# Output projection's first tiles inside the end of attention, and the embeddings' second operands in tiles of their own

## The chip, the cores and the metric

The kernel runs on one core of one Trainium2 chip. The metric is the time of one execution on the device in microseconds: 3075.62 us, the median of three runs (3073.82 to 3077.36). Lower is better.

## The reference

Two layers of an encoder over 1024 tokens of width 1024, all in fp32. Layer 0 mixes tokens by two groups of heads side by side (dilated windows, and attention with latent keys and values), layer 1 by differential attention. With `mix(x)` the heads' outputs side by side, a layer is

```
x <- LN(alpha*x + mix(x) @ W_o)          # output projection, then layer norm
x <- LN(alpha*x + convGLU(x))
x <- x + sigmoid(x @ W_g) * (p[i] @ W_p) # per-layer embeddings, p[i] is 1024 x 256
```

The change touches the last attention items of both layers, the output projection behind them, and `p[i] @ W_p`, which is worked out ahead of time among the last attention items.

## The kernel before, in words

**Operands.** For a product in fp32, each operand is split into a rounded high part (`...h`) and a low remainder (`...l`), and each block is three matmuls: high by high, high by low, low by high (`mm3`, L159 to L161). `split` (L146, or L139 by `pool_copy`) makes the high part on GpSimd (POOL) or, where the call says so, on ScalarE (ACT); the low part is a subtraction on VectorE (DVE, L149). `load_split` (L153) loads a matrix into a raw tile and splits it. Raw tiles of a region come in two rotating buffers. At the end of attention they serve, in turn, the embeddings' operands `wpr` and `ppr`, the eight weights of the output projection `wor` (tiles `woh`, `wol` after the split), and the mix rows `mr` (`mhl` after the split). A load waits on SP, the queue that issues transfers, until the low part of the buffer's last user is made.

**Attention.** A layer's attention is a row of items, 128 in layer 0 and 64 in layer 1; one is a head and a tile of 128 query rows. `a()` makes scores `s`, the row maximum `nmx` on DVE, and the exponential `e` on ACT (L440) with its sum. In layer 0, `r` (a reciprocal on DVE) and a multiplication on POOL (L740) norm `e`; in layer 1, two exponentials are combined with POOL (L845) and DVE (L846). `b()` transposes `e` on TensorE into `xt` (L164) and splits that to `pth`, `ptl`. `c()`, once for two items, multiplies by the values into `av` (L447, L448), and `d()` writes the outputs `oT`. `pipeline` calls these in an order one item apart, and runs at each item's slot what a plan has put there. `last_plan` fills that plan for the last head: the load of the embeddings' operands, 16 products `pe` of 128 x 512, the eight weights, and, at the last slot (`end - MT_SLOT[i]`, with zero for both layers), the load and split of the mix rows of tile 0 (`MixTiles.seven`, seven of eight heads; the last head comes from `oT`).

**Output projection.** `out_proj` goes over eight tiles of 128 tokens. A tile is 48 matmuls (8 heads, 2 halves of 512, 3 products) into one of the two PSUM buffers of two banks, which it shares with the attention scores (`banks2`). Behind it come the residual (DVE, L1078), the sums of the layer norm (DVE, L892; their sum L895; POOL L896 and L897 for the root), two passes on DVE (L902, L903) and one on POOL (L904), a store `xmid`, and in `xt.put` eight transposes of `xn` (L164) with their splits `xb` on ACT and DVE, which feed the next stage. The transposes of tile t - 1 are written behind the matmuls of tile t.

**Order.** Each engine runs its own list in a fixed order. A scheduler of the framework sets these lists from the order of the code and its own estimates. The two rotating raw buffers, and the pools' buffers in general, decide which instruction waits for which.

Of the kernel before, what the change touches and what calls it, by code (L numbers as in the profile page):

```python
# [15 lines left out]
P = 128  # L16
NT = 8
NK = 8
# [5 lines left out]
LAM_INIT = 0.8 - 0.6 * math.exp(-0.3)  # L24
N_UNITS = 36
PE_SLOTS = ((15, 5, 0), (6, 1, 0))
MT_SLOT = (0, 0)
DOWN = ("a00", "s4", "a01", "s2", "s3", "s1", "a11")
AHEAD = 3

# [2 lines left out]
def tile_hybrid_encoder(  # L33
# [32 lines left out]
    nc = tc.nc  # L66
# [33 lines left out]
    region = [None]  # L100
# [24 lines left out]
    def banks2(s):  # L125
        return ps.tile([P, 1024], F32, tag="s", name=nm(s), bufs=2)
# [21 lines left out]
            pool_copy(h, raw)  # L148
        (lo or nc.vector).tensor_tensor(l, raw, f32(h), op=ALU.subtract)  # L149

    def load_split(dram, shape, s, make=runit, hi=None, lo=None):
        r = region[0].raw(s + "r", shape)
        nc.sync.dma_start(out=r, in_=dram)  # L153
        h, l = make(s + "h", shape), make(s + "l", shape)
        split(r, h, l, hi, lo)
        return h, l
# [311 lines left out]
            for step in self.at.get((slot, place), ()):  # L468
                step()

    def pipeline(items, plan):


        n = len(items)
        items[0].prep()
        items[1].prep()
        items[2].prep()
        plan.run(-1, "first")
        items[0].a()
        plan.run(-1, "last")  # L480
        pending = ended = None
        for i in range(n):
            plan.run(i, "first")
            if i + 1 < n:
                items[i + 1].a()
            if i + 3 < n:
                items[i + 3].prep()
            plan.run(i, "mid")
            if ended is not None:
                ended.d()  # L490
                ended = None
            if pending is not None:
                pending.c()
                pending, ended = None, pending
            items[i].b()
            if items[i].t % 2 == 1:
                pending = items[i]
            plan.run(i, "last")
        pending.c()
        pending.d()  # L500

# [405 lines left out]
    class MixTiles:  # L907

        def __init__(self, i):
            self.i, self.m = i, {}  # L910

        def seven(self, t):

            mr = region[0].raw("mr", [P, NK, P])
            nc.sync.dma_start(out=mr[:, 0:7, :], in_=mix[self.i].rearrange("k p q -> p k q")[:, 0:7, t * P:(t + 1) * P])
            two = [runit("mhl", [P, 2, 4, P]) for _ in range(2)]
            for j, m in enumerate(two):
                n = 4 - j
                split(mr[:, 4 * j:4 * j + n], m[:, 0, 0:n], m[:, 1, 0:n])
            self.m[t] = mr, two  # L920

        def last(self, t, oT):
            mr, two = self.m[t]
            x = oT[:, t * P:(t + 1) * P]
            split(x, two[1][:, 0, 3], two[1][:, 1, 3], nc.scalar)
            self.m[t] = [(two[k // 4][:, 0, k % 4], two[k // 4][:, 1, k % 4]) for k in range(NK)]

    def last_plan(plan, i, first, end):


        w, wp, pp = [], [], []

        def load():
            new_region(4)
            for k in range(2):
                wp.append(load_split(w_pp[i, k], [P, 1024], "wp", rtile))
                pp.append(load_split(pT_in[i, :, k, :], [P, 1024], "pp", rtile if k == 0 else runit))

        def project(t, n):
            ts, sl = slice(t * P, t * P + P), slice(512 * n, 512 * n + 512)  # L940
            pe = bank("pe")
            for k in range(2):
                mm3(pe, pp[k][0][:, ts], pp[k][1][:, ts], wp[k][0][:, sl], wp[k][1][:, sl], k == 0, k == 1)
            for h in range(2):
                o = mid1("peo", [P, 256])
                nc.scalar.copy(o, pe[:, 256 * h:256 * h + 256])
                nc.sync.dma_start(out=pes[i][t, :, 512 * n + 256 * h:512 * n + 256 * h + 256], in_=o)

        def weight(k):
            w.append(load_split((w_abo, w_co)[i][k], [P, 1024], "wo", rtile if k > 4 else runit))  # L950

        mid, late, hold = PE_SLOTS[i]
        plan.add(first - 1, "mid", load)
        for t in range(NT):
            for n in range(2):
                j = 2 * t + n
                slot = end if j >= 16 - hold else first + j * mid // (16 - hold)
                plan.add(slot, "mid", lambda t=t, n=n: project(t, n))
        for k in range(NK):
            plan.add(first + late + k * (end - first - late) // NK, "mid", lambda k=k: weight(k))  # L960
        mt = MixTiles(i)
        plan.add(end - MT_SLOT[i], "mid", lambda: mt.seven(0))
        return w, mt

    def mixer_ab(xt):
        mask = big("mask", [P, 1664])
        st = {}
        last = {}

        def sink(i):  # L970
            def f(oT):
                if i < 7:
                    nc.sync.dma_start(out=mix[0][i], in_=oT)
                last["oT"] = oT
            return f

        ablk = [Block64(xt, w_a[i], True) for i in range(4)]
        new_region(3)
        xt.begin(0, ablk[0])
        for t in range(1, 4):  # L980
            xt.load(t)
        xt.split(1)
        rope_tables()
        for t in range(NT):
            if t + 4 < NT:
                xt.load(t + 4)
            if t == 2:
                constants()
            if t == 4:
                nc.sync.dma_start(out=mask, in_=mask_in)  # L990
            if t + 2 < NT:
                xt.split(t + 2)
            ablk[0].project(t, 2)
        ablk[0].keys(NT - 2)
        cT = Latent(xt)
        grp = [GroupB(cT, g) for g in range(2)]
        bblk = [BlockB(cT, grp[i // 2], i) for i in range(4)]
        items, plan = [], Plan()
        for i in range(4):
            sti = {"sink": sink(i)}  # L1000
            items += [ItemA(ablk[i], j, t, mask, sti) for j in range(2) for t in range(NT)]
            if i < 3:
                ablk[i + 1].plan(plan, 16 * i - 1, 2)
            else:
                plan.add(16 * i - 1, "mid", lambda: cT.load(384, w_cq))
                plan.spread(cT.steps() + bblk[0].steps(), 16 * i, 16 * i + 13)
                plan.add(16 * i + 14, "mid", lambda: bblk[0].keys(NT - 1))
        for i in range(4):
            sti = {"sink": sink(4 + i)}
            items += [ItemB(bblk[i], j, t, sti) for j in range(2) for t in range(NT)]  # L1010
            if i < 3:
                plan.spread(bblk[i + 1].steps(), 64 + 16 * i, 64 + 16 * i + 13)
                plan.add(64 + 16 * i + 14, "mid", lambda i=i: bblk[i + 1].keys(NT - 1))
            else:
                w, mt = last_plan(plan, 0, 112, 127)
        plan.add(-1, "first", lambda: ablk[0].keys(NT - 1))
        plan.add(-1, "last", lambda: ablk[1].load(True), lambda: ablk[1].project(0))
        pipeline(items, plan)
        return w, mt, last["oT"]

    def mixer_c(xt, late):
# [24 lines left out]
                w, mt = last_plan(plan, 1, 56, 63)  # L1046
        plan.add(-1, "first", lambda: blk[0].keys(NT - 1))
        plan.add(-1, "last", lambda: blk[1].load(True), lambda: blk[1].project(0))
        pipeline(items, plan)
        return w, mt, last["oT"]  # L1050


    def out_proj(i, w, mt, oT, xsrc, xt, early):

        ln = LN(ln_mg[i], ln_mb[i])
        xns, m = [], mt.m

        def load(t):
            if t < NT:
                if t not in m:  # L1060
                    mt.seven(t)
                mt.last(t, oT)
# [3 lines left out]
            nc.sync.dma_start(out=xns[t], in_=xsrc[t])  # L1066

        def linear(t, beside=None):

            xr, mt_ = xns[t], m.pop(t)  # L1070
            po = banks2("po")
            for k in range(NK):
                if k == NK // 2 and beside:
                    beside()
                for n in range(2):
                    sl = slice(512 * n, 512 * n + 512)
                    mm3(po[:, sl], *mt_[k], w[k][0][:, sl], w[k][1][:, sl], k == 0, k == NK - 1)
            nc.vector.scalar_tensor_tensor(xr, xr, ALPHA, po, op0=ALU.mult, op1=ALU.add)  # L1078

        load(0)  # L1080
        for t in range(NT):
            residual(t)
            load(t + 1)
            if t < NT - 1:
                linear(t)
            else:
                early(0)
                linear(t, lambda: early(1))
                ln(xns[t], True)
                nc.sync.dma_start(out=xmid[i][t], in_=xns[t])  # L1090
            if t:
                xt.put(t - 1, xns[t - 1])
            if t < NT - 1:
                ln(xns[t], t == NT - 2)
                nc.sync.dma_start(out=xmid[i][t], in_=xns[t])
# [624 lines left out]
```

## Time and profile before

| | us |
|---|---|
| median of three runs | 3075.62 (3073.82 to 3077.36) |
| profiled execution | 3070.2, of it the span 3068.4 |
| TensorE busy | 2956.1 (96% of the span) |
| VectorE busy | 2339.5 (76%) |
| ScalarE, GpSimd busy | 1239.0, 1110.6 |
| mean granted TensorE clock | 0.99 of full speed |
| end of layer 0's attention, its output projection | about 690 to 704, 703 to 812 |
| layer 1's embeddings | about 2116 to 2180 |
| end of layer 1's attention, its output projection | about 2180 to 2200, 2195 to 2307 |

A row of the timeline has the start, the duration, the engine, the line, the operation with its tiles by the program's names, the shapes, and the count where equal instructions follow each other. In brackets stands the time for which the engine had been idle before it and what ended that. PE is TensorE, SPq the queue of transfers. Matmuls overlap, so the time from one start to the next is shorter than the duration shown. A row of windows has the length, the busy time of PE, its weight loads, DVE, ACT and POOL with counts, the granted clock, and the share and rate of transfers.

### The profile page before, as it was taken

The page shows a single profiled execution, that of the slowest core. Times are in us where ns is not written, and L with a number is a line of the kernel's source. Part 1 is how long each engine was busy: PE and PEld are TensorE (multiplying, and loading weights), DVE is VectorE, ACT ScalarE, POOL GpSimd, SP SyncE. Part 2 cuts the span into 40 slices and gives each one's busy share as a digit, 9 for nine tenths or more (in the row PEclk, how much of TensorE's full clock was granted, in tenths as well). Part 3 has the DMA queues.
Part 4 walks back from the last instruction along what each step waited for, and adds up shares of the span by engine and source line. Part 5 has one row for each costly group of instructions (what it writes and reads, how often), then busy time and mean ns, then how long its engine had stood idle before and what let it go on. Part 6 is the DMA issues. An engine that isn't in the chain of part 4 may idle for free.

```text
span 3068.4 us, 43192 instructions
## 1 busy us (share of the span) xinstructions
PE 2956.1 (96%) x15456; PEld 2535.4 (83%) x15456; DVE 2339.5 (76%) x4014; ACT 1239.0 (40%) x2652; POOL 1110.6 (36%) x1646
## 2 busy tenths in 40 slices
PE   8999999999889999999999999999998999999989
PEld 8888989887778888877788999998776888887877
DVE  6676477876898888788638777777779988879674
ACT  5555477761232222223226555555413322222221
POOL 4444544333232222234225555554333222213232
PEclk9999999999999999999999999999998999999999
DMA  3000100033223232734111100001532232255331
GB/s 122 29 28 19 38 29 8 22 118 130 96 103 103 99 106 106 283 112 168 56 59 36 35 28 29 28 18 62 174 108 86 103 103 103 103 201 198 97 137 65
DMA packets 119718, 272.14 MB, mean 89 GB/s; under 512 B 11344, under 2 KB 35024, under 8 KB 119504
## 3 DMA queue, kind: packets, MB, share of 16 engines
q1 hardware_dynamic: 119504, 269.37, 25.6%
q8 instruction: 123, 2.02, 0.3%
q14 instruction: 91, 0.75, 0.1%
HBM read 196.46 MB, written 72.88 MB: 88 GB/s over the span
## 4 chain that ended last, share of the span: by engine, by line
PE 70%; DVE 16%; issue 6%; POOL 3%; ACT 3%; DMA 2%; SPq 0%; POOLq 0%; DVEq 0%; ACTq 0%
PE xt L164 5%; PE pb L159 5%; PE pb L160 5%; PE pb L161 5%; PE pp L159 4%; PE s L588 4%; PE pp L161 4%; PE pp L160 4%; PE pd L160 2%; PE pd L161 2%; PE pd L159 2%; PE pa L159 2%; PE pg L159 2%; PE pa L161 2%; PE pa L160 2%
## 5 line engine op out<-in xcount | busy, mean ns | idle before, releaser
L142 DVE TENSOR_TENSOR ptl<-xt,pth 128x512 fp32r<-128x512 f32 (+2 forms) x384 | 239.7, 652 | 59.2 <-ACT pth L399 42.6
L159 PE MATMUL pp<-wh,xth 128*128 128x384 f32 x768 | 266.3, 347 | 7.9 <-ACT wh L146 7.4
L160 PE MATMUL pp<-wl,xth 128*128 128x384 f32 x768 | 258.8, 337 | 1.9 <-DVE wl L149 1.9
L161 PE MATMUL pp<-wh,xtl 128*128 128x384 f32 x768 | 257.9, 336 | 0.0
L440 ACT ACTIVATE e<-s,nmx 128x1024 f32<-128x1024 f32 x192 | 214.7, 1120 | 81.4 <-DVE nmx L838 58.7
L160 PE MATMUL pd<-wd,gd 128*128 128x512 f32 x616 | 242.4, 393 | 4.2 <-DVE wd L142 4.2
L159 PE MATMUL pd<-wd,gd 128*128 128x512 f32 x616 | 241.0, 391 | 0.0
L161 PE MATMUL pd<-wd,gd 128*128 128x512 f32 x616 | 240.5, 390 | 0.0
L139 POOL TENSOR_SCALAR wd<-wd 128x512 fp32r<-128x512 f32 x154 | 129.9, 848 | 290.8 <-PE pd L161 215.6
L1149 ACT CAST gd<-gr 128x512 fp32r<-128x512 f32 x154 | 94.8, 622 | 312.2 <-PE pd L161 222.0
L325 ACT CAST w<-ws 128x512 fp32r<-128x512 f32 x132 | 81.2, 621 | 336.8 <-PE pb L161 281.2
L164 PE MATMUL xt<-ident,e 128*128 128x128 f32 x1440 | 198.0, 274 | 10.0 <-POOL e L740 3.0
L159 PE MATMUL pb<-xt,w 128*128 128x512 f32 x528 | 207.0, 392 | 0.0
L160 PE MATMUL pb<-xt,w 128*128 128x512 f32 x528 | 206.5, 391 | 0.0
L161 PE MATMUL pb<-xt,w 128*128 128x512 f32 x528 | 206.3, 391 | 0.0
L139 POOL TENSOR_SCALAR w<-ws 128x512 fp32r<-128x512 f32 x44 | 33.4, 761 | 467.1 <-PE pa L161 416.9
L164 PEld LDWEIGHTS xt<-ident,e 128*128 128x128 f32 x1440 | 163.4, 141 | 30.7 <-ACT sq L870 5.9
L142 DVE TENSOR_TENSOR wd<-wd,wd 128x512 fp32r<-128x512 f32 x154 | 112.3, 731 | 68.8 <-POOL wd L139 68.8
L142 DVE TENSOR_TENSOR w<-ws,w 128x512 fp32r<-128x512 f32 x176 | 152.4, 869 | 5.2 <-ACT w L325 3.2
L159 PEld LDWEIGHTS pp<-wh,xth 128*128 128x128 f32 x768 | 144.6, 188 | 13.4 <-ACT wh L146 8.0
L838 DVE TENSOR_REDUCE nmx<-s 128x1 f32<-128x1024 f32 x128 | 150.4, 1213 | 1.7 <-PE s L588 1.6
L159 PE MATMUL pb<-xb,w 128*128 128x512 f32 x352 | 140.2, 398 | 9.8 <-DVE u L1330 5.7
(293 smaller groups left out, 8864.5 us busy)
## 6 DMA issues: line engine op xcount, KB each, us to landing
gr<-gated SPq DMA_DIRECT2D x76, 512.0 KB, 3.7
gated<-c SPq DMA_DIRECT2D x90, 256.0 KB, 3.7
wf<-in_w_gate_dram SPq DMA_DIRECT2D x44, 512.0 KB, 4.0
wf<-in_w_up_dram SPq DMA_DIRECT2D x44, 512.0 KB, 4.1
wd<-in_w_down_dram SPq DMA_DIRECT2D x44, 512.0 KB, 6.0
wr<-in_w_c_dram SPq DMA_DIRECT2D x32, 384.0 KB, 3.2
gated<-u SPq DMA_DIRECT2D x44, 256.0 KB, 2.2
pes<-peo SPq DMA_DIRECT2D x64, 128.0 KB, 1.9
```

The source lines that it names most:

```text
L139: nc.gpsimd.tensor_scalar(o, i, 1.0, 1.0, op0=ALU.mult, op1=ALU.mult)
L142: nc.vector.tensor_tensor(lo, src, f32(hi), op=ALU.subtract)
L159: nc.tensor.matmul(o, lhsT=lh, rhs=rh, start=start, stop=False)
L160: nc.tensor.matmul(o, lhsT=lh, rhs=rl, start=False, stop=False)
L161: nc.tensor.matmul(o, lhsT=ll, rhs=rh, start=False, stop=stop)
L164: nc.tensor.transpose(o, in_=i, identity=ident)
L325: nc.scalar.copy(h, v)
L440: nc.scalar.activation(dst, s, AF.Exp, bias=negmax, scale=1.0, accum_out=l)
L588: nc.tensor.matmul(s[:, kh * 512:kh * 512 + 512], lhsT=qt[:, hl, i, :], rhs=self.ks[kh][:, j, :], start=hl == 0, stop=hl == 1)
L838: nc.vector.tensor_reduce(out=nmx, in_=s, axis=AX.X, op=ALU.max, negate=True)
L1149: nc.scalar.copy(g[:, 0], rg)
```

## The change

Two things change. First, the output projection's work starts inside the attention. The mix rows of tile 0 are loaded two slots earlier and those of tile 1 at the last slot. `pipeline` takes a function `tail`: heads 0 to 3 of tile 0 (24 matmuls) are written ahead of the last item's transposes, heads 4 to 6 (18) ahead of the last pair's values. Behind the attention, heads 0 to 6 of tile 1 (42) come first, then head 7 of tile 0, then head 7 of tile 1; later tiles are as before. Second, the embeddings' second operands are loaded into tiles of the unit pool and no longer into the rotating raw buffers; the high part of the second weight moves from POOL to ACT, and the tile pools of the second `pp` stay as they were.

```diff
-MT_SLOT = (0, 0)
...
-    def load_split(dram, shape, s, make=runit, hi=None, lo=None):
-        r = region[0].raw(s + "r", shape)
+    def load_split(dram, shape, s, make=runit, hi=None, lo=None, raw=None):
+        r = (raw or region[0].raw)(s + "r", shape)
...
-    def pipeline(items, plan):
+    def pipeline(items, plan, tail):
...
+            if i == n - 1:
+                tail(0)
             items[i].b()
             if items[i].t % 2 == 1:
                 pending = items[i]
             plan.run(i, "last")
+        tail(1)
         pending.c()
         pending.d()
...
+        def part(self, t, ks):
+
+            if t not in self.po:
+                self.po[t] = banks2("po")
+            for k in ks:
+                h, l = (self.two[t][k // 4][:, a, k % 4] for a in range(2))
+                for n in range(2):
+                    sl = slice(512 * n, 512 * n + 512)
+                    mm3(self.po[t][:, sl], h, l, self.w[k][0][:, sl], self.w[k][1][:, sl], k == 0, k == NK - 1)
+
+        def tail(self, n):
+
+            self.part(0, range(4) if n == 0 else range(4, 7))
...
             for k in range(2):
-                wp.append(load_split(w_pp[i, k], [P, 1024], "wp", rtile))
-                pp.append(load_split(pT_in[i, :, k, :], [P, 1024], "pp", rtile if k == 0 else runit))
+                raw = unit if k else None
+                wp.append(load_split(w_pp[i, k], [P, 1024], "wp", rtile, nc.scalar if k else None, raw=raw))
+                pp.append(load_split(pT_in[i, :, k, :], [P, 1024], "pp", runit if k else rtile, raw=raw))
...
-        plan.add(end - MT_SLOT[i], "mid", lambda: mt.seven(0))
+        plan.add(end - 2, "mid", lambda: mt.seven(0))
+        plan.add(end, "mid", lambda: mt.seven(1))
+        mt.w = w
...
         def linear(t, beside=None):
-
-            xr, mt_ = xns[t], m.pop(t)
-            po = banks2("po")
-            for k in range(NK):
-                if k == NK // 2 and beside:
+            xr = xns[t]
+            if t > 1:
+                mt.part(t, range(4))
+                if beside:
                     beside()
-                for n in range(2):
-                    sl = slice(512 * n, 512 * n + 512)
-                    mm3(po[:, sl], *mt_[k], w[k][0][:, sl], w[k][1][:, sl], k == 0, k == NK - 1)
+                mt.part(t, range(4, 7))
+            mt.part(t, (7,))
+            m.pop(t)
+            po = mt.po.pop(t)
             nc.vector.scalar_tensor_tensor(xr, xr, ALPHA, po, op0=ALU.mult, op1=ALU.add)
...
             load(t + 1)
+            if t == 0:
+                mt.part(1, range(7))
```

The line numbers of the profile are those of the kernel before; in the changed kernel the splits and matmuls stand one line higher, the layer norm two lower, and the residual at L1096. Three places of the instruction order show what moves.

GpSimd at the end of layer 0's attention, before (the last three weights, `e` of the last two items, the mix rows of tile 0 and tile 1):

```order
L740 TENSOR_SCALAR e_9440<-e_9440,r_9438 128x1024
L139 TENSOR_SCALAR woh_9334<-wor_9332 128x1024
L139 TENSOR_SCALAR woh_9387<-wor_9385 128x1024
L740 TENSOR_SCALAR e_9488<-e_9488,r_9486 128x1024
L139 TENSOR_SCALAR woh_9459<-wor_9457 128x1024
L139 TENSOR_SCALAR mhl_9545<-mr_9543 128x512
L139 TENSOR_SCALAR mhl_9546<-mr_9543 128x384
```

and now:

```order
L742 TENSOR_SCALAR e_9440<-e_9440,r_9438 128x1024
L138 TENSOR_SCALAR woh_9334<-wor_9332 128x1024
L138 TENSOR_SCALAR woh_9387<-wor_9385 128x1024
L138 TENSOR_SCALAR woh_9459<-wor_9457 128x1024
L138 TENSOR_SCALAR mhl_9465<-mr_9463 128x512
L138 TENSOR_SCALAR mhl_9466<-mr_9463 128x384
L742 TENSOR_SCALAR e_9496<-e_9496,r_9494 128x1024
```

The last item's `e` has moved behind the last weight and the mix rows of tile 0. On TensorE its transposes have 24 matmuls of tile 0 ahead of them.

TensorE in layer 0's output projection, around the transposes of tile 0's `xn`, before (`po_9676` is tile 1, `po_9776` tile 2):

```order
L159 MATMUL po_9676<-woh_9459,mhl_9595 128x512
L160 MATMUL po_9676<-wol_9460,mhl_9595 128x512
L161 MATMUL po_9676<-woh_9459,mhl_9595 128x512
L164 MATMUL xt_9734<-ident,xn_9590 128x128 x4
L164 MATMUL xt_9743<-ident,xn_9590 128x128 x4
L159 MATMUL po_9776<-woh_8950,mhl_9668 128x512
```

and now:

```order
L160 MATMUL po_9776<-woh_9133,mhl_9711 128x512
L158 MATMUL po_9776<-woh_9257,mhl_9712 128x512
L159 MATMUL po_9776<-wol_9258,mhl_9712 128x512
L163 MATMUL xt_9734<-ident,xn_9641 128x128 x4
L163 MATMUL xt_9743<-ident,xn_9641 128x128 x4
L160 MATMUL po_9776<-woh_9257,mhl_9712 128x512
```

The transposes stand 26 matmuls into tile 2; tile 0 itself now ends six matmuls before tile 1 does. Those of tile 1's `xn` stand 14 matmuls into tile 3, those of tile 2's 4 into tile 4, and from tile 3 on the order is as before. Layer 1 has the same.

VectorE there, before (`xn_9590` is tile 0, `xn_9664` tile 1):

```order
L1078 SCALAR_TENSOR_TENSOR xn_9590<-xn_9590,po_9602 128x1024
L892 BN_STATS st_9652<-xn_9590 128x6 x2
L895 BN_AGGR mv_9653<-st_9652 128x2
L902 TENSOR_SCALAR xn_9590<-xn_9590,mv_9653,rs_9654 128x1024
L903 TENSOR_TENSOR xn_9590<-xn_9590,lngb_9585 128x1024
L1078 SCALAR_TENSOR_TENSOR xn_9664<-xn_9664,po_9676 128x1024
L142 TENSOR_TENSOR xb_2369_9728<-xt_9734,xb_2367_9726 128x2x128
```

and now (tile 0 is `xn_9641`, tile 1 `xn_9707`):

```order
L1096 SCALAR_TENSOR_TENSOR xn_9641<-xn_9641,po_9559 128x1024
L894 BN_STATS st_9695<-xn_9641 128x6 x2
L1096 SCALAR_TENSOR_TENSOR xn_9707<-xn_9707,po_9645 128x1024
L897 BN_AGGR mv_9696<-st_9695 128x2
L904 TENSOR_SCALAR xn_9641<-xn_9641,mv_9696,rs_9697 128x1024
L905 TENSOR_TENSOR xn_9641<-xn_9641,lngb_9636 128x1024
L141 TENSOR_TENSOR xb_2369_9728<-xt_9734,xb_2367_9726 128x2x128
```

The residual of tile 1 stands inside the layer norm of tile 0, between its sums and their sum; the sums of tile 1 follow the splits of tile 0's transposes in both.

More of the change, by code (lines that the diff above doesn't have):

```diff
@@ L909, in __init__ @@
         def __init__(self, i):
-            self.i, self.m = i, {}
+            self.i, self.m, self.two, self.po = i, {}, {}, {}
+        def part(self, t, ks):
[8 more added lines that the diff above has]
+            self.part(0, range(4) if n == 0 else range(4, 7))
         def seven(self, t):
@@ L919, in seven @@
                 split(mr[:, 4 * j:4 * j + n], m[:, 0, 0:n], m[:, 1, 0:n])
-            self.m[t] = mr, two
+            self.m[t] = self.two[t] = two
         def last(self, t, oT):
-            mr, two = self.m[t]
+            two = self.two[t]
             x = oT[:, t * P:(t + 1) * P]
             split(x, two[1][:, 0, 3], two[1][:, 1, 3], nc.scalar)
-            self.m[t] = [(two[k // 4][:, 0, k % 4], two[k // 4][:, 1, k % 4]) for k in range(NK)]
     def last_plan(plan, i, first, end):
@@ L1017, in mixer_ab @@
         plan.add(-1, "last", lambda: ablk[1].load(True), lambda: ablk[1].project(0))
-        pipeline(items, plan)
+        pipeline(items, plan, mt.tail)
         return w, mt, last["oT"]
@@ L1048, in mixer_c @@
         plan.add(-1, "last", lambda: blk[1].load(True), lambda: blk[1].project(0))
-        pipeline(items, plan)
+        pipeline(items, plan, mt.tail)
         return w, mt, last["oT"]
```

## The prediction

> **What bounds the kernel now.** I read the page's first two parts, then TensorE's timeline around the three places that the change touches, then those of the engines that release it there.
>
> ```profile
> span 3068.4 us, 43192 instructions
> PE 2956.1 (96%) x15456; PEld 2535.4 (83%) x15456; DVE 2339.5 (76%) x4014; ACT 1239.0 (40%) x2652; POOL 1110.6 (36%) x1646
> 694.24 1.04 PE L164 MATMUL xt<-ident,e 128*128 128x128 f32 x8
> 697.57 1.10 PE L164 MATMUL xt<-ident,e 128*128 128x128 f32 x8 [2.29 <-POOL e L740]
> 698.90 0.39 PE L447 MATMUL av<-pth,v 128*128 128x256 f32 x1 [0.24 <-ACT pth L399]
> 699.63 0.38 PE L448 MATMUL av<-ptl,v 128*128 128x256 f32 x1 [0.34 <-DVE ptl L142]
> 702.60 0.63 PE L159 MATMUL po<-woh,mhl 128*128 128x512 f32 x1
> 2185.86 0.63 PE L164 MATMUL xt<-ident,e 128*128 128x128 f32 x4 [2.75 <-ACT e L440]
> 2193.28 1.09 PE L164 MATMUL xt<-ident,e 128*128 128x128 f32 x8 [2.06 <-DVE e L846]
> 2133.39 1.38 PE L159 MATMUL pe<-wph,pph 128*128 128x512 f32 x3 [1.03 <-POOL pph L139]
> ```
>
> TensorE is busy 96% of the span, so only what fills or opens its gaps counts. The gaps meant here are short: 2.87 us at layer 0's last item (2.29 + 0.24 + 0.34), 4.81 in the two rows of layer 1's, 1.03 for the second operand of the embeddings. One more resource shows in the granted clock, by windows of 3.41 us:
>
> ```profile
> 696.73:700.14 3.41, 1.99 (x13) 1.56 (x14) 2.53 (x5) 1.27 (x3) 1.83 (x2) 1.00 0.90 287
> 700.14:703.56 3.42, 3.42 (x16) 3.23 (x16) 2.88 (x5) 0.70 (x3) 1.31 (x2) 0.50 0.58 180
> 2130.33:2133.74 3.41, 1.31 (x5) 0.79 (x6) 3.41 (x4) 1.21 (x2) 2.37 (x2) 1.00 0.31 119
> 2133.74:2137.15 3.41, 3.41 (x9) 2.46 (x8) 3.27 (x4) 0.10 (x1) 0.00 (x0) 0.50 0.48 155
> 2181.53:2184.94 3.41, 1.58 (x9) 1.07 (x7) 3.41 (x6) 1.86 (x5) 2.01 (x1) 1.00 0.54 127
> 2184.94:2188.35 3.41, 2.22 (x17) 2.01 (x18) 3.41 (x5) 0.82 (x2) 1.04 (x1) 1.00 0.88 284
> ```
>
> (After the colon pair: length, busy PE, PEld, DVE, ACT, POOL, then the clock.) After windows with gaps the clock is 0.50 for one window, which costs 1.7 us; 1.31 us of work brought it on, 1.58 us in layer 1 did not.
>
> **Layer 0's end of attention.** New there: 24 matmuls of tile 0 ahead of the last item's transposes. They need the mix rows.
>
> ```profile
> 696.18 0.38 SPq L915 DMA_DIRECT2D mr<-mix  x1
> 693.52 2.63 DVE L149 TENSOR_TENSOR wol<-wor,woh 128x1024 fp32r<-128x1024 f32 x2
> 701.33 2.33 SPq L915 DMA_DIRECT2D mr<-mix  x2
> 700.95 1.31 POOL L139 TENSOR_SCALAR mhl<-mr 128x512 fp32r<-128x512 f32 x2 [1.32 <-DMA mr<-mix]
> 705.08 1.10 POOL L139 TENSOR_SCALAR mhl<-mr 128x512 fp32r<-128x512 f32 x2 [2.82 <-DMA mr<-mix]
> ```
>
> The load of the mix rows waits for a raw slot, which weight 6's low part frees at 696.15. Two planner slots earlier do not move that: the issue stays at 696.18, the rows are there 4.77 us later. Their first hi half is split by 700.95 + 0.65 = 701.6. So TensorE, free of transposes at 695.03 (694.24 and eight steps of 0.1, as from 724.87 to 725.66 below), stands 6.6 us; the third matmul waits another 0.45 for DVE's low half; and the window to 703.56 runs at half clock, 0.75 more: 7.8 lost. Before, 702.60 - 695.03 = 7.57 held eight transposes (0.8) and 16 av matmuls of half the width of po's (0.12 each), 2.7 us at full clock, so 4.9 were lost, and 0.4 to 703.56: 5.3. **+2.5 us**. The last e, now behind both mix splits on POOL, comes at about 704.3 (702.3, the two low parts and r on DVE, 1.1 for e). The 24 matmuls last 5.5 us, to 707 and more (48 from 725.66 to 736.79 give 0.23 a step), so it is late for nobody. Bounds: +2.0 if the rows land in 3.75 us, as the next tile's do, from the issue at 701.33 to the split at 705.08; +4.2 with a second half-clock window.
>
> By the Trainium skill (TensorE: Matmul & The Clock Gate, Part 1: The HAM clock gate) the clock halves after an idle window of about 3.4 us; a standstill of 6.6 contains one, so rule and row make the same half-clock window, and it cannot be saved here.
>
> **Layer 1's end.**
>
> ```profile
> 2182.15 0.33 SPq L153 DMA_DIRECT2D wor<-in_w_co_dram  x1
> 2183.31 1.21 DVE L838 TENSOR_REDUCE nmx<-s 128x1 f32<-128x1024 f32 x1
> 2184.55 1.11 ACT L440 ACTIVATE e<-s,nmx 128x1024 f32<-128x1024 f32 x1 [1.54 <-DVE nmx L838]
> 2193.74 1.48 DVE L149 TENSOR_TENSOR mhl<-mr,mhl 128x512 fp32r<-128x512 f32 x2
> ```
>
> Here the order of loads puts the mix rows ahead of weight 7, into its issue at 2182.15: landed at 2185.9 to 2186.9, hi 0.65 later, both low parts (1.48) done at 2188.0 to 2189.1. They now stand ahead of both nmx of the last item on DVE, and tile 0's PSUM buffer is the one whose scores the first of these exponentials reads. So nmx (1.21) and e (1.11) come first: first po at 2190.4 to 2191.4, its 24 end around 2196.4, and e for the last transposes (second nmx, e, POOL, DVE: about 2195.4) is ready by then. Before, these transposes began at 2193.28 with no po done: 2193.28 + 5.5 - 2196.4 = **-2.4 us** (-2.9 to -1.9).
>
> **Embeddings.** In layer 1 the second operands are loaded at once; their splits no longer wait for a slot and the 1.03 us gap goes. The window with 1.31 us of work would then hold 2.3, more than the 1.58 which kept the clock: 1.7 more. DVE's two splits of 1.2 us now precede an nmx, but the second nmx of that item stood behind both already, and e needs the two. **-2.5 us** (-2.7 to -1.0). In layer 0 there is little to win:
>
> ```profile
> 620.22 1.09 PE L164 MATMUL xt<-ident,e 128*128 128x128 f32 x8 [0.54 <-POOL e L740]
> 625.35 0.50 PE L159 MATMUL pe<-wph,pph 128*128 128x512 f32 x1 [0.29 <-DVE ptl L142]
> ```
>
> 0 (-0.8 to +0.5; the loss is an ACT split of the kind that stands ahead of an exponential).
>
> **Out projection: the large term.** 42 matmuls of tile 1 stand ahead of tile 0's last six. Tile 0 thus ends 9.6 us (42 steps of 0.23) later in TensorE's work, and with it the LN chain starts later, while the transposes of xn0 follow after 6 + 26 matmuls in place of 48.
>
> ```profile
> 713.75 0.39 PE L161 MATMUL po<-woh,mhl 128*128 128x512 f32 x1
> 714.18 1.22 DVE L1078 SCALAR_TENSOR_TENSOR xn<-xn,po 128x1024 f32<-128x1024 f32 x1 [4.42 <-PE po L161]
> 720.06 2.42 POOL L904 TENSOR_TENSOR xn<-xn,lngb 128x1024 f32<-128x1024 f32 x1 [2.19 <-DVE xn L903]
> 724.87 1.04 PE L164 MATMUL xt<-ident,xn 128*128 128x128 f32 x8
> 725.66 0.47 PE L159 MATMUL po<-woh,mhl 128*128 128x512 f32 x1
> 728.60 1.28 DVE L892 BATCH_NORM_STATS2 st<-xn 128x6 f32<-128x512 f32 x2
> 733.95 2.78 POOL L904 TENSOR_TENSOR xn<-xn,lngb 128x1024 f32<-128x1024 f32 x1 [2.26 <-DVE xn L903]
> 736.79 1.09 PE L164 MATMUL xt<-ident,xn 128*128 128x128 f32 x8
> 741.73 1.27 DVE L892 BATCH_NORM_STATS2 st<-xn 128x6 f32<-128x512 f32 x2
> 747.48 2.38 POOL L904 TENSOR_TENSOR xn<-xn,lngb 128x1024 f32<-128x1024 f32 x1 [2.26 <-DVE xn L903]
> 749.91 1.09 PE L164 MATMUL xt<-ident,xn 128*128 128x128 f32 x8 [1.10 <-POOL xn L904]
> 757.27 2.41 POOL L904 TENSOR_TENSOR xn<-xn,lngb 128x1024 f32<-128x1024 f32 x1 [2.19 <-DVE xn L903]
> 2244.37 1.10 PE L164 MATMUL xt<-ident,xn 128*128 128x128 f32 x8 [0.71 <-POOL xn L904]
> ```
>
> The chain feeds itself: BN of tile t+1 stands on DVE behind the splits of xt(t). Call S the start of tile 0's last matmul (713.75 here).
> - xn0: done at 722.48, S + 8.7; tile 1's residual (1.22, 1.1 with overlap) now lies between BN and its sum, so S + 9.9. TensorE is there at S + 0.43 + 1.22 (po2 needs tile 0's PSUM buffer) + 26 x 0.23 = S + 7.6. Stall 2.3.
> - xn1: from xt0 at 724.87 to 736.73 is 11.9 (xt1 followed 0.06 later: no slack even now); with the residual gone from it I take 11.6. Between the two TensorE now has eight transposes (0.8) and 22 + 14 matmuls, 9.0. Stall 2.6.
> - xn2: 736.79 to 749.86 is 13.1; BN then begins as early as after xt0 (3.7, not 4.9) and two mix splits move behind it (+0.3): 12.2. TensorE has 0.8 + 38 matmuls, 9.5. Stall 2.7.
> - xn3: 9.8 (749.91 to 759.68) against 0.8 + 44 matmuls, 10.8: none, and from there the order is as before.
>
> 7.6 of stalls replace 1.10 in layer 0 and 0.71 in layer 1: +6.5 and +6.9, **+13.4 us**. Bounds: 4.0 a layer if the chain ran at the 9.8 to 10.6 of tiles with few mix splits (+6.2), 9.0 with nothing saved in xn2 (+16.2).
>
> **Clock at the new stalls.** A stall of 2.6 us can leave under 1.4 us of work in a window. Lost time ahead of xt1 and xt2 is taken up by their stalls; behind the third half of 1.7 us per layer may count, twice at even odds: **+1.0** (0 to +3.4). The same page of the Trainium skill (HAM oscillation) sets the harm at pauses above about 3.4 us; by it this term is 0 and the sum 11.0. The window from 2130.33 held 1.31 us of work in 3.41, so no pause in it was above 2.1 us, and the clock fell all the same: row and rule differ, and I keep my term.
>
> **Sum.** 2.5 - 2.4 - 2.5 + 0 + 13.4 + 1.0 = +12.0 us. The profiled execution took 3070.2 us (its span 3068.4 and 1.8 around it), 5.4 under the median of 3075.62; the change goes on either: 3082 for a profiled execution like it, **3087.6** for the median. The outer ends of all terms are +1.8 and +21.4.
>
> **Rivals.**
> - *The chain gives way*: the DVE, with mix splits done in its free time, runs xn1 and xn2 as xn3 (9.8), and tile 1's residual costs nothing (8.7): stalls 1.1 + 0.8 + 0.3, +1.3 a layer, and no clock term: 2.5 - 2.4 - 2.5 + 2.6 = +0.2, 3076. For: the xt2 to xn3 rows. Against: the order leaves the mix splits of tiles 3 to 5 between the BN rows. This decides as soon as the chain per tile is below some 10 us.
> - *The fill works*: the mix rows are there when the fill begins, all gaps of both ends close (-5.3 with the slow clock in layer 0, -4.8 in layer 1), the embeddings give 3.5 (2.7 + 0.8), the chain as in the first rival: -11.0, 3065. It needs an issue before 691; the row says 696.18 and the slot it waits for is the same.
> - *The clock falls at each stall*, and again at layer 0's end: +12.0 + 1.7 (the second window there) + 2.4 (the rest of the clock term) + some 2 where stalls do not absorb it, +18: 3094. For: each stall leaves about 0.8 us of work in a window that holds it whole. Against: the 2.75 us gap of layer 1 fell across two windows, and neither lost its clock.
> - The change not doing what it says is part of the forecast: in layer 0 the filler itself waits.
>
> **Chances.** Forecast (+7 to +17) 0.62, chain gives way 0.20, fill works 0.06, clock 0.12. The chain gets its fifth because xn2's 12.2 and xn1's 11.6 rest on DVE rows that stand differently now. A measurement of this kernel tells apart some 0.2%, 6.15 us. Slower by more: 0.62 + 0.12, 0.74; within: 0.20, the first rival; faster 0.06. The range for 8 in 10 leaves out the fill, the lower part of the first rival and the far end of the clock: 3075 to 3094; the forecast's own is 3082.5 to 3093.
>
> **What would show it.** In layer 0: first po at about 701.6, POOL's last e behind it, clock 0.50 around it. In layer 1: first po near 2191 released by ACT's e. No pph row ahead of pe. In each out projection three xt rows with 2.3 to 2.7 us before them, released by POOL's xn. It is wrong if those xt follow without idle time, or if the first po of layer 0 starts near 697.

## The result, and the profile after

The changed kernel takes 3092.09 us (3090.24 to 3096.48, four runs), the kernel before, measured with it, 3076.02 (3073.82 to 3077.36, four runs): 16.1 us more. The ratio is 1.0055, with a 95% interval of 1.0038 to 1.0072. The change made the kernel slower, by 12 to 22 us by this interval.

The page of the changed kernel, first part:

```profile
span 3094.7 us, 43213 instructions
PE 2965.8 (96%) x15456; PEld 2543.5 (82%) x15456; DVE 2340.3 (76%) x4014; ACT 1240.9 (40%) x2654; POOL 1110.3 (36%) x1644
```

DVE, ACT and POOL are busy for as long as before. TensorE shows 9.7 us more of busy time for the same 15456 matmuls, which is what half clock looks like in a busy column, and the rest of the longer span is idle time.

End of layer 0's attention in the changed kernel, the timelines of TensorE, POOL and SP:

```profile
696.23 1.04 PE L163 MATMUL xt<-ident,e 128*128 128x128 f32 x8
703.76 0.79 PE L158 MATMUL po<-woh,mhl 128*128 128x512 f32 x1 [6.50 <-POOL mhl L138]
703.08 1.09 POOL L138 TENSOR_SCALAR mhl<-mr 128x512 fp32r<-128x512 f32 x2 [1.22 <-DMA mr<-mix]
705.36 1.12 POOL L742 TENSOR_SCALAR e<-e,r 128x1024 f32<-128x1024 f32 x1 [1.18 <-DVE r L741]
698.16 7.41 SPq L931 DMA_DIRECT2D mr<-mix  x3
```

The filler waits 6.50 us for the mix rows: issued at 698.16, split from 703.08, with the issue still behind weight 6, whose low part ends at 698.13. Before, TensorE had idled 2.87 us here. The last `e` comes after the splits and is late for nobody. The windows of the changed kernel, with the columns as before:

```profile
699.41:702.82 3.41, 0.00 (x0) 0.00 (x0) 0.93 (x1) 0.17 (x1) 1.05 (x1) 0.50 0.62 201
702.82:706.24 3.42, 2.48 (x6) 1.68 (x7) 2.77 (x7) 0.00 (x0) 1.98 (x3) 0.50 0.45 134
706.24:709.65 3.41, 3.41 (x10) 2.64 (x9) 2.37 (x5) 0.00 (x0) 1.52 (x4) 0.50 0.94 296
709.65:713.06 3.41, 3.41 (x21) 2.88 (x19) 1.45 (x2) 0.23 (x1) 0.91 (x2) 1.00 0.97 304
2143.25:2146.66 3.41, 1.71 (x7) 0.76 (x5) 3.06 (x6) 0.18 (x1) 2.29 (x2) 1.00 0.84 280
2146.66:2150.07 3.41, 2.61 (x6) 2.13 (x7) 3.41 (x5) 0.00 (x0) 0.00 (x0) 0.50 0.05 22
2266.13:2269.54 3.41, 2.47 (x10) 2.38 (x11) 0.48 (x2) 0.84 (x3) 0.88 (x1) 0.50 0.38 154
2269.54:2272.95 3.41, 3.41 (x9) 2.63 (x9) 2.52 (x6) 0.55 (x2) 0.58 (x2) 0.50 0.00 0
```

Half clock lasts three windows, 5.9 us of it with TensorE at work (703.76 to 709.65), which costs 2.9 us. The window from 702.82 held 2.48 us of busy time, and the next was slow all the same; so was the one after 2266.13, with 2.47. Of the two rows from the embeddings of layer 1, the first ran at full clock with 1.71 us of busy time, and half clock followed it.

The transposes of `xn` in the two output projections of the changed kernel, TensorE's timeline:

```profile
739.47 1.09 PE L163 MATMUL xt<-ident,xn 128*128 128x128 f32 x8 [1.75 <-POOL xn L906]
750.73 1.10 PE L163 MATMUL xt<-ident,xn 128*128 128x128 f32 x8 [1.98 <-POOL xn L906]
763.69 1.46 PE L163 MATMUL xt<-ident,xn 128*128 128x128 f32 x8 [3.21 <-POOL xn L906]
776.25 1.03 PE L163 MATMUL xt<-ident,xn 128*128 128x128 f32 x8
2241.30 1.09 PE L163 MATMUL xt<-ident,xn 128*128 128x128 f32 x8 [1.75 <-POOL xn L906]
2252.57 1.09 PE L163 MATMUL xt<-ident,xn 128*128 128x128 f32 x8 [1.98 <-POOL xn L906]
2267.07 1.97 PE L163 MATMUL xt<-ident,xn 128*128 128x128 f32 x8 [4.75 <-POOL xn L906]
2280.77 1.04 PE L163 MATMUL xt<-ident,xn 128*128 128x128 f32 x8
```

Three stalls per layer, each released by POOL's last pass over `xn`: 6.94 us in layer 0 and 8.48 in layer 1, where there were 1.10 and 0.71. The fourth transposes wait for nothing. The third stall of layer 1 is the longest, and POOL's rows before it (with the load that they wait for, from SP) show a link of the chain that the first two lack:

```profile
2253.97 0.37 SPq L931 DMA_DIRECT2D mr<-mix  x1
2259.63 0.62 POOL L138 TENSOR_SCALAR mhl<-mr 128x512 fp32r<-128x512 f32 x1 [5.31 <-DMA mr<-mix]
2260.33 0.70 POOL L898 TENSOR_SCALAR rs<-mv 128x1 f32<-128x1 f32 x1
```

A split of a later tile's mix rows stands on POOL ahead of `rs`, the layer norm's root, and waits for its load. The sums that `rs` needs (`mv`, DVE) were ready at 2257.57, so the root came 2.8 us late. In layer 0 the same split waited 3.78 us, and the root came 1.2 us late.

End of layer 1's attention (TensorE, ACT) and the embeddings' second product (TensorE, DVE, POOL), changed kernel:

```profile
2200.25 0.39 PE L159 MATMUL av<-ptl,v 128*128 128x256 f32 x1 [0.93 <-DVE ptl L141]
2205.21 0.70 PE L871 MATMUL ss<-sq,ones 128*128 128x256 f32 x2 [0.64 <-ACT sq L864]
2206.97 0.47 PE L158 MATMUL po<-woh,mhl 128*128 128x512 f32 x1 [1.06 <-POOL woh L138]
2206.67 0.19 ACT L439 ACTIVATION_READ_ACCUMULATOR e<-s,nmx 128x1 f32 x1
2147.46 0.79 PE L158 MATMUL pe<-wph,pph 128*128 128x512 f32 x1 [2.04 <-DVE ptl L141]
2144.75 2.05 DVE L848 SCALAR_TENSOR_TENSOR e<-e,r,e 128x1024 f32<-128x1024 f32 x1 [0.35 <-POOL e L847]
2144.68 1.05 POOL L138 TENSOR_SCALAR pph<-ppr 128x1024 fp32r<-128x1024 f32 x1
```

At layer 1's end the gaps are 2.6 us for 4.8 before. The bracket at 2206.97 names a POOL split; but the matmul starts 0.11 us after the sum of ACT's exponential has been read out (2206.67 + 0.19). That exponential reads scores from PSUM buffers that `po` shares, and in both kernels with early mix rows below the bracket of the first `po` names it (2.54 us, `ACT e`); so I take it to have released the matmul here too. At the embeddings, the gap before `pph` is gone, but the wait before the next product has grown from 1.26 to 2.04 us: DVE's row took 2.05 us, not 1.28, while POOL split `pph`.

### The profile page after: what moved, and what is told of

The parts are those of the page before. It is cut to its first block, busy times and chain, and to the rows that moved or that the text cites. A ratio compares the mean times of both kernels' runs of the same rounds, so it can differ in the third digit from the quotient of the medians.

```text
span 3094.7 us, 43213 instructions
## 1 busy us (share of the span) xinstructions
PE 2965.8 (96%) x15456; PEld 2543.5 (82%) x15456; DVE 2340.3 (76%) x4014; ACT 1240.9 (40%) x2654; POOL 1110.3 (36%) x1644
## 4 chain that ended last, share of the span: by engine, by line
PE 72%; DVE 14%; issue 5%; POOL 3%; ACT 3%; DMA 2%; SPq 0%; POOLq 0%; DVEq 0%; ACTq 0%
PE xt L163 5%; PE pb L158 5%; PE pb L160 5%; PE pb L159 5%; PE pp L158 4%; PE pp L159 4%; PE pp L160 4%; PE s L590 4%; PE pd L159 2%; PE pd L160 2%; PE pd L158 2%; PE pa L158 2%; PE pa L159 2%; PE pa L160 2%; PE pg L158 2%
## 5 line engine op out<-in xcount | busy, mean ns | idle before, releaser
L439 ACT ACTIVATE e<-s,nmx 128x1024 f32<-128x1024 f32 x192 | 214.8, 1120 | 67.7 <-DVE nmx L840 49.3
L398 ACT CAST pth<-xt 128x512 fp32r<-128x512 f32 x256 | 142.8, 594 | 25.9 <-PE xt L163 23.5
```

The lines of the kernel that those rows point to most:

```text
L398: nc.scalar.copy(self.h[b][:, :, sl], pt)
L439: nc.scalar.activation(dst, s, AF.Exp, bias=negmax, scale=1.0, accum_out=l)
```

## The experiments

Times are medians against the kernel before, measured in the same series; a difference "by the ratio" is the table's ratio times the time before. The first question was which part of the change makes the +16.1 us.

| kernel | median, us | before, us | ratio, 95% interval |
|---|---|---|---|
| changed kernel | 3092.09 | 3076.02 | 1.0055 (1.0038 to 1.0072) |
| no matmul of tile 1 ahead of tile 0's end | 3071.72 | 3076.80 | 0.9989 (0.9981 to 0.9998) |
| 12 of the 42 | 3073.15 | 3076.80 | 0.9987 (0.9978 to 0.9996) |
| 24 of the 42 | 3080.11 | 3076.14 | 1.0011 (1.0002 to 1.0020) |
| embeddings' part alone | 3072.28 | 3076.80 | 0.9989 (0.9981 to 0.9998) |
| change without the embeddings' part | 3090.62 | 3076.80 | 1.0053 (1.0041 to 1.0066) |
| mix rows early, all 42 | 3088.86 | 3076.14 | 1.0042 (1.0028 to 1.0055) |
| mix rows early, none of the 42 | 3072.58 | 3076.14 | 0.9985 (0.9977 to 0.9994) |
| the same, pph split on ACT | 3074.21 | 3076.14 | 0.9993 (0.9985 to 1.0002) |
| transfer early, splits 2 slots before the end | 3068.10 | 3077.55 | 0.9967 (0.9956 to 0.9979) |
| transfer early, splits 1 slot before the end | 3067.88 | 3077.55 | 0.9971 (0.9959 to 0.9983) |
| transfer early, splits 2 and 1 slots before the end | 3064.32 | 3075.56 | 0.9964 (0.9950 to 0.9977) |

**No hoist.** Tile 1 goes back behind tile 0; all else as changed.

```diff
             if t == 0:
-                mt.part(1, range(7))
+                pass
 ...
+            if t == 1:
+                mt.part(1, range(0, 7))
             if t > 1:
```

> Tile 1's 42 matmuls go back behind tile 0's end; the tails inside the attention and the embeddings stay as changed. Theory (order of the out projection): tile 0 ends 9.6 us earlier in TensorE's work, so the stalls at the transposes of xn0, xn1 and xn2 (6.94 us in layer 0, 8.48 in layer 1 of the changed profile) fall back to the 1.10 and 0.71 of before, 13.6 us less, and the half-clock windows behind them (some 4.6 us) go too; new is a wait of 1.5 to 2 us per layer for the split of the last head, which nothing covers. Of the 16.1 us lost some 14 come back: +2 us against the kernel before (0 to +5). Rival 1 (the filler's wait for the mix rows is the whole loss): no change, +16 us. Rival 2 (the chain gave way and the clock is the loss): about half comes back, +8 us.

Measured: -5 us against before by the medians, -3.4 by the ratio (0.6 to 5.8 faster), so all of the loss and more comes back. TensorE's timeline in this kernel, all rows with idle time from the end of layer 0's attention to the fourth transposes, and the one row of layer 1's output projection before its sixth:

```profile
703.64 0.79 PE L158 MATMUL po<-woh,mhl 128*128 128x512 f32 x1 [6.07 <-POOL mhl L138]
754.63 1.09 PE L163 MATMUL xt<-ident,xn 128*128 128x128 f32 x8 [0.70 <-POOL xn L906]
2243.51 1.10 PE L163 MATMUL xt<-ident,xn 128*128 128x128 f32 x8 [0.71 <-POOL xn L906]
```

The stalls at `xn` are back to 0.70 and 0.71, while the filler still waits 6.07 us. The theory of the order holds and the filler's wait alone does not make the loss. One thing was expected wrongly: the wait of 1.5 to 2 us for the last head's split does not exist. Tile 0 needs the last head's output for the first 128 tokens, which an early item makes, not the last one. So the 42 matmuls covered nothing.

**12 and 24 of the 42.** As above with `range(2)` or `range(4)` in front, and the rest behind.

> Only 12 of tile 1's 42 matmuls stay ahead of tile 0's last six (2.7 us of cover). Theory: cover enough for the last head's split, and tile 0's norm has 36 matmuls (8.4 us) for a chain of 8.7: a stall of about 0.3 at the first transposes, 1.10 and 0.71 later as before. 2 to 4 us faster than the kernel with no hoist, -1 us against the kernel before (-4 to +2). Rival 1 (the filler's wait is the loss): +16. If the number of matmuls ahead of tile 0's end did not matter, this kernel and the one without a hoist would differ by the missing wait alone and both stand near +16.

> 24 of the 42 matmuls stay ahead of tile 0's last six (with none -4.7 us, with 12 -3.7 us, with all 42 +16.1 against the kernel before). Theory (a chain of 8.7 us from tile 0's end to xn0, then 11.9 per tile): the first transposes come 24 + 3 matmuls behind tile 0's end, 6.4 us, a stall of 2.3; the second after 45, 11.1 us for a chain of 11.9, a stall of 0.8; the third as before: 3 us per layer more than with 12, some +2.5 us (0 to +5). Rival (a threshold: the loss comes only with the fragments of tiles 3 and 4): as with 12, -4.

Measured: with 12, -4 us (the expected -1 was too cautious by the wait that isn't there), which these runs can't tell from the kernel with none; with 24, +4 by the medians and +3.4 by the ratio, as expected within its range. The first two transposes of `xn` in layer 0, with 12 (first row) and in the next fence with 24:

```profile
730.69 1.09 PE L163 MATMUL xt<-ident,xn 128*128 128x128 f32 x8 [0.22 <-POOL xn L906]
```

```profile
731.47 1.09 PE L163 MATMUL xt<-ident,xn 128*128 128x128 f32 x8 [2.19 <-POOL xn L906]
743.16 1.09 PE L163 MATMUL xt<-ident,xn 128*128 128x128 f32 x8 [0.35 <-POOL xn L906]
```

0.3 and 2.3 had been worked out for the first transposes from the chain of 8.7 us; 0.22 and 2.19 were measured. With 24, the transposes of tile 1's `xn` and the later ones stand at tile ends again, not inside tiles 3 and 4 (the fragments of the rival), and the loss is there already, so it does not come with the fragments alone.

**Each part alone.** The embeddings' part on the kernel before, and the change without it.

> The kernel before with the embeddings' second operands in tiles of their own, nothing else. By the trace after: layer 1 +0.9 us from the pp matmuls to the end of the embeddings (idle 4.24 for 4.35, half clock 3.02 for 1.71), layer 0 -0.3: +0.5 us, not to be told from no change (-2 to +2). By the prediction's term: -2.5 us (-3.5 to -1.0).

> The change without its embeddings part. Theory: the tails and the out projection carry the whole loss, +15.5 us (+12 to +19) against the kernel before; with the prediction's embeddings term it would be +18.5.

Measured: the tails and the output projection carry the loss (+14 us by the medians, +16 by the ratio); the embeddings alone win 3.4 us by the ratio (0.6 to 5.8), the size of the prediction's term and not what the trace after had led me to expect. In the profile of the embeddings alone, the stretch from the `qt` transposes at 2112.59 to the sums behind the products at 2180.33 is 67.7 us for 68.0 before (2111.70 to 2179.65), and layer 0's second small wait (0.29) is gone. That is some 0.6 us; where the rest of the 3.4 lies isn't shown. The mechanism of the prediction's term isn't in that profile either: the 1.03 us gap went, but the wait before the next product grew from 1.26 to 2.04 us, and the half-clock window stayed (from 2132.95). Nor does the win show inside the change: with and without the embeddings part it stands at 1.0055 and 1.0053 of before, with intervals that overlap.

**Mix rows early.** In their own raw tile, loaded and split 8 slots before the end in layer 0 and 5 in layer 1; first with all 42, then with none.

```diff
-        def seven(self, t):
+        def seven(self, t, raw=None):
 
-            mr = region[0].raw("mr", [P, NK, P])
+            mr = (raw or region[0].raw)("mr", [P, NK, P])
 ...
-        plan.add(end - 2, "mid", lambda: mt.seven(0))
+        plan.add(end - (8, 5)[i], "mid", lambda: mt.seven(0, unit))
```

> The changed kernel with its 42 matmuls kept, but the mix rows of tile 0 go to a raw tile of the unit pool and are loaded 8 slots before the end in layer 0, 5 in layer 1. Theory (two losses that add): the fill of layer 0 starts right behind the transposes, so the 6.5 us before it and the three half-clock windows (2.9 us) go, the stalls at the three xn transposes of each layer stay at 1.7 to 4.8: 9 us less than the changed kernel, +7 us against the kernel before (+4 to +9). Rival 1 (the fill's wait is the loss): faster than before by some 5 us, -5. Rival 2 (TensorE only waits elsewhere, for the last e): +13 or more.

> The same early mix rows, and none of tile 1's matmuls ahead of tile 0's end; embeddings as changed. Theory: the kernel without a hoist stands at -4.7 us against the kernel before; its wait of 6.07 us for the mix rows in layer 0 and two half-clock windows (2.9 us) go, and in layer 1 some 0.5 to 1 us: -13 us (-15 to -9), 3063 us. Rival (the last e becomes the next wait in layer 0, since the scores, not the mix rows, are late): 2 us more, -8.

Measured: +13 us with all 42, -5 us by the ratio (-4 by the medians) with none. The filler's wait in layer 0 is gone in both, and the stalls at `xn` stay in the first (1.74, 1.98 and 1.89 us in layer 0, 1.74, 1.98 and 1.64 in layer 1), as the theory has it. But of the wins of 9 and 8 us that were expected, some 4 and 1 us came by the ratios, which the intervals barely tell from none. With none of the 42, these rows tell where it went (TensorE in both layers, DVE and POOL in layer 1):

```profile
671.39 0.31 PE L163 MATMUL qt<-ident,q 128*96 128x128 f32 x1 [1.57 <-DVE qt L141]
672.91 0.50 PE L158 MATMUL pe<-wph,pph 128*128 128x512 f32 x1 [0.97 <-DVE oT L451]
2167.24 0.76 PE L158 MATMUL pe<-wph,pph 128*128 128x512 f32 x1 [3.47 <-DVE ptl L141]
2162.79 1.85 POOL L138 TENSOR_SCALAR mhl<-mr 128x512 fp32r<-128x512 f32 x2 [1.98 <-DMA mr<-mix]
2164.20 2.29 DVE L148 TENSOR_TENSOR mhl<-mr,mhl 128x512 fp32r<-128x512 f32 x2 [0.51 <-POOL mhl L138]
```

POOL waits for rows that were requested 4.6 us before (issue at 2158.13), DVE waits for POOL and then works 2.29 us, and the splits of transposes that TensorE needs stand behind. The wait had only moved, with a half-clock window in layer 0 and two in layer 1. The rival named for this run (the last `e` in layer 0) was not it, since no transposes of `e` wait there. In the run with all 42, the +13 is the number of its second rival, but there too layer 0's last items wait no more than 0.19 us for an `e`.

**pph on ACT.** The same kernel, with `nc.scalar` for the split of the second `pph`.

> As the kernel with early mix rows and no hoist, with the high part of the second embedding operand (pph) made on ACT in place of GpSimd. Theory (DVE's e row took 2.05 us in place of 1.28 because GpSimd split pph during it): the row in layer 1 is 1.28 again, the wait of 2.04 us at the embeddings' second product 1.3, and its window may keep its clock: 0.8 to 3.8 us less than without the move. Rival (the longer row has another cause): 2.05 and 2.04 as before, same time. Against the kernel before: -15 us (-18 to -11).

Measured: the two rows came out as expected in layer 1 (DVE, then TensorE, in this kernel):

```profile
2136.07 1.28 DVE L848 SCALAR_TENSOR_TENSOR e<-e,r,e 128x1024 f32<-128x1024 f32 x1 [0.35 <-POOL e L847]
2138.01 0.50 PE L158 MATMUL pe<-wph,pph 128*128 128x512 f32 x1 [1.27 <-DVE ptl L141]
```

So POOL's split beside it had made the DVE row longer. The time did not follow: 3074.21, no better than the kernel without this edit. In layer 0 the move made a new wait of 1.10 us (TensorE, for the low part of the same operand).

**Transfer early, splits late.** The load apart from the split: requested 8 and 5 slots before the end into the own raw tile, split two slots or one before the end.

```diff
-        plan.add(end - 2, "mid", lambda: mt.seven(0))
+        plan.add(end - (8, 5)[i], "mid", lambda: mt.fetch(0, unit))
+        plan.add(end - (2, 2)[i], "mid", lambda: mt.seven(0))
```

> As the kernel with early mix rows and no hoist, but only the transfer is early (8 and 5 slots before the end, own raw tile); the splits of the mix rows stay two slots before the end. Theory: with the splits early too, DVE stood behind them for rows that had just been requested (3.47 us in layer 1's embeddings, 1.57 and 0.97 in layer 0), and this gave back what the fill won; with the splits late the rows have long landed, so these waits go and the fill's wait of 6.07 us and its half clock stay away: 8 us less than the kernel without a hoist (-4.7 against before), -12 us against the kernel before (-14 to -8). Rival (DVE and POOL are full there, whatever they wait for, so the splits cost the same where they stand): -4.

> The same with the splits one slot before the end. Theory: in layer 0 the mix rows' low parts now stand behind two weights on DVE, so the first of the 24 matmuls waits some 2 us; in layer 1 the last item's row maxima stand ahead of the splits. -10 us against the kernel before (-13 to -6). Rival (no gain from early rows at all): -4.

Measured: -10 and -9 us by the ratio; the theory's sizes were -12 and -10. The two can't be told apart by these times. In the kernel with two slots, layer 0 has no idle time from its last items to the third transposes of `xn`; layer 1 has a new wait, for the DVE row that combines the exponentials, behind the first split:

```profile
2184.45 1.09 PE L163 MATMUL xt<-ident,e 128*128 128x128 f32 x4 [3.99 <-DVE e L848]
```

With one slot, layer 0 waits 1.25 us for the low part, and this row is absent.

**Each layer its own slot.** `(2, 1)` in place of `(2, 2)`.

> The splits of the mix rows two slots before the end in layer 0 and one before it in layer 1, all else as in the two kernels with the early transfer. Theory: each layer takes the better of the two. From the last items to the fourth transposes of xn, layer 0 took 62.4 us with two slots and 65.1 with one (67.5 in the kernel before), layer 1 78.1 with two and 75.5 with one (76.6 before): 2.6 us less than either of the two kernels (-9.5 us against before), -12 us (-14 to -9). Rival (the scheduler's order around the splits changes with every slot, and what one layer wins the run does not keep): -9.

Measured: 3064.32 us (3062.16 to 3066.89, five runs), 0.9964 of before: -11 us, against an expected -12. Its median is the lowest of all; by the ratios it is 1 and 2 us ahead of the two kernels it joins, less than the intervals, so that it beats them isn't shown, and the rival's -9 lies inside its interval. At the two ends of attention its profile shows no gap in layer 0 and three short ones in layer 1 (0.93, 0.78 and 0.85 us), and no half-clock window at either.

## Why the prediction was right, point by point

The forecast was +12.0 us for the median; it was +16.1, inside the range, and nearer to the +18 of the rival with the clock than to the forecast's own sum. By its steps, the profiled executions compared (idle time from the brackets; for the clock, half of the time that TensorE worked at 0.50):

- **Layer 0's end**, +2.5: measured 6.50 for 2.87 us of idle time, and 2.9 for 1.7 us of clock, +4.9. The place, the standstill (6.6 us forecast) and the cause (the raw slot behind weight 6) were right. The mis-sized term is the clock: I took one half-clock window, and it was three: one without any work, one with 2.48 us of busy time, which did not end it, and one busy throughout. I had that as the upper bound (+4.2), and even there with one window too few.
- **Layer 1's end**, -2.4: 2.63 us of idle time in the gaps shown for the 4.81 quoted before, and with the small gaps 2.7 for 5.4, so -2.7. The first `po` came right behind ACT's exponential, as forecast.
- **Embeddings**, -2.5: by these two executions +0.9; alone, by the times, -3.4. The 1.03 us gap went, as forecast. That the sizes agree may be luck, since the half-clock window stands in both profiles, the changed kernel's and that of the embeddings alone. The step that missed is "1.7 more" for the clock: I took the windows' work from the gap alone and overlooked that POOL's split, no longer waiting, falls on DVE's row and makes it 0.77 us longer. Nor was 1.58 us of work in a window a limit: the first row of windows in the prediction, from 696.73, has 1.99, and half clock follows it; here 1.71 lost it (from 2143.25). Whether a window of half clock came then seems to have hung on where it began: without the 42 matmuls the same gaps (1.61, 0.44, 2.03 us) had no slow window.
- **Output projection**, +13.4: 6.94 - 1.10 and 8.48 - 0.71, +13.6. The single stalls were 1.75, 1.98 and 3.21 for 2.3, 2.6 and 2.7 in layer 0, and 1.75, 1.98 and 4.75 in layer 1. So the mechanism was right, and that 13.6 meets 13.4 is partly luck: the chain was 0.6 us quicker than I had it at the first two, and at the third 0.5 and 2.1 us longer. What I had left out there is POOL's split of mix rows ahead of the root, which waits for a load (3.78 and 5.31 us). The dose of 0, 12, 24 and 42 matmuls (-5, -4, +4, +16 us by the medians) shows that tile 0's late end is the cause.
- **Clock at the new stalls**, +1.0: 1.7 in layer 0 (the window from 764.26) and 2.9 in layer 1 (two windows, with little idle time in them), +4.6. The count of windows failed here too: the term was too small. The Trainium skill (TensorE: Matmul & The Clock Gate, HAM oscillation) puts the harm at pauses above about 3.4 us. Layer 1's stall of 4.75 us is such a pause; layer 0's of 3.21 is not, and the clock fell behind it as well.

The parts add up to 4.9 - 2.7 + 0.9 + 13.6 + 4.6 = 21.3 us, the two profiled executions differ by 26.3 and the medians by 16.1. Of the 26.3, 2.4 have arisen by 577 us, ahead of every changed instruction. The profiled execution of before was among its fastest (3070.2, with a median of 3076), the one of after its slowest. Idle time alone gives 3.6 - 2.7 - 0.1 + 13.6 = 14.4, closer to the medians; which half-clock windows fall into a given execution is not the same from one to the next (the mean granted clock of the kernel before lay between 0.986 and 0.991 over its executions).

Of the rivals, the chain did not give way, the fill did not work, and the clock came in part: windows fell behind the third stalls and doubled at layer 0's end. The chance that I gave it (0.12) was low for what the clock did.

## What to carry to other kernels

Before work is put ahead of a tile's last matmuls, follow what starts at that tile's end: here a layer norm over three engines, whose pace per tile was already TensorE's, so 9.6 us of matmuls in front of it came back as 7 to 8.5 us of stalls in each layer. A load placed earlier in the code is no earlier if its buffer rotates behind the same user; give it a buffer of its own, request it early, and leave the instructions that wait for it where its data have long landed, since every engine here runs its list in a fixed order, and such an instruction holds up all that stands behind it (3.47 us in layer 1's embeddings). And ask of a filler what it covers: this one stood ahead of six matmuls that, without it, had nothing to wait for.

## What the runs showed of the hardware

- At half clock, windows with 2.47, 2.48 and 2.61 us of busy time (from 2266.13, 702.82 and 2146.66 us of the changed kernel) were followed by another slow one, while one with 1.58 us at full clock had kept it. That is more busy time, but it is not shown to be more work: from one `po` matmul to the next it took 0.43 us at half clock and 0.23 at full, so 2.61 us there are some 1.4 us of work at full clock. These slow stretches ended behind a window in which TensorE was busy throughout (from 2269.54, 706.24 and 2150.07); in the change without its embeddings part, one window with 2.72 us sufficed (from 761.77).
- At full clock, busy time alone did not decide whether a window of 3.41 us was followed by half clock. One with 1.47 us was not (the kernel with 24 of the 42, from 1577.11), nor the one with 1.58; ones with 1.71 (changed kernel, from 2143.25), 1.99 (before, from 696.73) and 2.01 (no hoist, from 290.45) were.
- A DVE row over two tensors of 128 x 1024 took 2.05 us beside a POOL split that started 0.07 us before it (changed kernel), and 1.28 when that split was on ACT; the POOL row took 1.05, as in the kernel before. Where the DVE row began first, by 0.15 us (splits 2 slots before the end, at 2183.02), it kept its 1.28 us, and POOL's split of a weight took 2.04. The Trainium skill (SBUF — State Buffer, SBUF: two separate sides) has it that VectorE and GpSimd share a port pair, which one of the two holds for its whole instruction and the other waits. The rows agree as to which of the two is held up; but DVE's row grew by 0.77 us where both ran for 0.98, so it did not wait for all of it.
